# Moving one modulation group of a two-block network from TensorE to VectorE, with earlier loads of the output slabs

## The chip, the cores and the metric

The kernel runs on one core of a Trainium2 chip. The metric is the device time of one execution in microseconds (us); less is better. Engines are named as the profile names them: PE is TensorE, DVE is VectorE, ACT is ScalarE, POOL is GpSimd, SP is SyncE, whose queue issues nearly all loads. In the views, L113 is the line of a helper through which almost every compute operation is recorded, so operations are told apart by the tiles they write and read (out<-in).

## The reference, cut to what matters

512 positions of 1024 channels pass through two blocks, all in fp32. The change lies in the first block, which is conditioned on a vector c:

```python
c_act = jax.nn.silu(c)
cond = c_act @ ada_w[i] + ada_b[i]
shift1, scale1, gate1, shift2, scale2, gate2 = jnp.split(cond, 6, axis=-1)
h = modulate(rmsnorm(x, norm1_g[i]), shift1, scale1)
z = h @ w_in[i] + b_in[i]
...
y = concatenate([rmsnorm(y_a, out_norm_a_g[i]), rmsnorm(y_b, out_norm_b_g[i])])
x = x + gate1 * (y @ w_out[i])
h2 = modulate(rmsnorm(x, norm2_g[i]), shift2, scale2)
g_ff, up_ff = split(h2 @ w_ffn_in[i], 2)
x = x + gate2 * ((silu(g_ff) * up_ff) @ w_ffn_out[i])
shift_f, scale_f = split(c_act @ ada_f_w + ada_f_b, 2)
return modulate(rmsnorm(x, norm_f_g), shift_f, scale_f)
```

The modulation vectors are products of one row (c_act, 1024) with a 1024 x 1024 matrix each. y_a is the spatial gating half of the mixer, y_b the convolution half (width 31, then a norm per channel group and silu). The second block (attention, pooling, two more feed-forward layers) is not touched.

## The kernel before, in words

**Products.** Every fp32 weight slab of 512 KB is loaded into a raw tile, split into a high part (wh, ScalarE) and a low part (wl, VectorE), and each product runs as three matmuls (wh with the high activations, wh with the low ones, wl with the high ones). `Weights` (L284 to L336) holds the plan of slabs: `load` (L296) issues the load on SyncE's queue, `take` gives the next split slab and splits ahead so that four are ready.

**Modulation.** Six groups of 8 slabs (each 128 x 1024 fp32, 512 KB) remain after the first norm: gate1, shift2, scale2, gate2, and the two of the last norm. `ada_fetch(n)` (L631) issues loads until n slabs are waiting. There are two ways to compute a group:

- `ada_group(ahead)` (L649), on TensorE: per slab four fp32 products in the program, which the profile lists as 8 matmul instructions (128x32 weights, 128x256 moving), 64 for a group, into one of the four PSUM banks `mm`; then `ada_columns` turns the row into columns by two transposes; then it fetches up to `ahead` slabs.
- `ada_slab(ahead=4)` (L663), on VectorE: per slab two 128x512 multiply-adds into the accumulator `adac`; after the eighth slab a short product with a matrix of ones (8 matmul instructions) and the same transposes.

**The stage around the change.** After the spatial gating (L1184), gate1 is computed by `ada_group` (L1188). The output projection is then made in two halves. The first-half products (L1193 to L1203) take the four channel blocks of y_a, for each of 8 output blocks m over all 512 positions; `gated` (L1179) scales each with gate1 and adds it to x on VectorE, which frees its `mm` bank. Between them `pump` issues the rest of the convolution: its taps, then centre, norm and silu of y_b, which go back and forth between VectorE, TensorE and ScalarE. At m = 2 shift2 and at m = 5 scale2 are computed by `ada_group`. The second-half products (L1214 to L1238) take y_b, whose operand tiles `HO.put(4 + k, ...)` (L1211) come last out of the convolution; they run over 256 positions at a time and use slabs 4 to 7 of `w_out`. scale2 is needed by `normed` (L534), near the end of this stage.

The feed-forward loop `Ffn.run` (L1091) then makes units m = 3 to 14 over all positions, and after each calls `ada_rest` (L1260), which works off two slabs of the last three groups by `ada_slab`.

**Order.** The program text gives the order of priority. The tile framework's scheduler (`tile.TileContext(nc, auto_bufs=True)`) works out each engine's instruction order from it and from its own estimates, chooses where in on-chip memory each tile lies, and makes a load wait until the last user of that place is done. [...]

Of the kernel before, what the change touches and what calls it, by code (L numbers as in the profile page):

```python
# [42 lines left out]
ADN = 10  # L43
# [77 lines left out]
def body(ctx: ExitStack, tc: tile.TileContext, I: dict, out, dbg=None):  # L121
# [12 lines left out]
    def A(name, dt=F32):  # L134
        tag, bufs = TAGS.get(name, ("m", NB))
        return ar.tile([P, 2, S], dt, tag=tag, name=name, bufs=bufs)
# [13 lines left out]
    def MM():  # L150
        return ps.tile([P, S], F32, tag="mm", name="mm", bufs=4)

    def ST():
        return ps.tile([P, S], F32, tag="st", name="st", bufs=2)
# [15 lines left out]
    def stt(o, a, s, b, op0, op1):  # L170
        return V.scalar_tensor_tensor(o, a, s, b, op0=op0, op1=op1)
# [4 lines left out]
    def ts(o, a, s, op, s2=None, op2=None):  # L176
        if op2 is None:
            return V.tensor_scalar(o, a, s, None, op0=op)
        return V.tensor_scalar(o, a, s, s2, op0=op, op1=op2)

    def dump(name, tiles):
        if dbg is not None and name in dbg:
            for k, t in enumerate(tiles):
                nc.sync.dma_start(dbg[name][:, k, :], t)
# [153 lines left out]
    W = Weights(4)  # L338
# [274 lines left out]
    def pump(n, m=0):  # L613
        owed[0] += n
        owed[1] += m
        n, m = int(owed[0]), int(owed[1])
        owed[0] -= n
        owed[1] -= m
        for j in range(max(n, m)):
            if j < m and bp:  # L620
                bp.popleft()()
            if j < n and bg:
                bg.popleft()()
# [7 lines left out]
    def ada_fetch(n):  # L631

        while adaq and len(adal) < n:
            w, c0, col, bias, k = adaq.popleft()
            a = A("adaw")
            nc.sync.dma_start(a.rearrange("p a c -> p (a c)"), w[k * P:(k + 1) * P, c0:c0 + D])
            adal.append((a, col, bias, k))

    def ada_columns(pq, col, bias):

        sb = T("adasb")
        act(sb[:, :HS], pq[:, :HS], AF.Copy)
        pt = ST()
        for t in range(2):
            TE.transpose(pt[:, t * P:(t + 1) * P], sb[:, t * P:(t + 1) * P], ident)
        v = pt[:, :HS].rearrange("p (t j r) -> p j t r", t=2, j=4)[:, :, :, 0]
        tt(mod[:, col:col + 8].rearrange("p (j t) -> p j t", t=2), v, vecs[bias[0]][:, bias[1]:bias[1] + 8].rearrange("p (j t) -> p j t", t=2), OP.add)

    def ada_group(ahead):  # L649

        pq = MM()
        for k in range(KD):
            ada_fetch(1)
            a, col, bias, _ = adal.popleft()
            for j in range(4):
                TE.matmul(pq[32 * j:32 * j + 32, :HS], lhsT=c32[:, k, :], rhs=a[:, j // 2, (j % 2) * HS:(j % 2 + 1) * HS],
                          start=(k == 0), stop=(k == KD - 1))
        ada_columns(pq, col, bias)
        ada_fetch(ahead)
# [3 lines left out]
    def ada_slab(ahead=4):  # L663

        ada_fetch(1)
        if not adal:
            return
        a, col, bias, k = adal.popleft()
        if k == 0:
            adac[0] = A("adac")  # L670
        acc = adac[0]
        for j in range(2):
            if k == 0:
                ts(acc[:, j], a[:, j], cact[:, k:k + 1], OP.mult)
            else:
                stt(acc[:, j], a[:, j], cact[:, k:k + 1], acc[:, j], OP.mult, OP.add)
        ada_fetch(ahead)
        if k == KD - 1:
            pq = ST()
            for j in range(4):  # L680
                TE.matmul(pq[32 * j:32 * j + 32, :HS], lhsT=ones[:, :32], rhs=acc[:, j // 2, (j % 2) * HS:(j % 2 + 1) * HS], start=True, stop=True)
            ada_columns(pq, col, bias)
# [242 lines left out]
    def factor(acc_, bank=ST):  # L925

        rsb = ACC()
        act(rsb, stats(acc_, 0, S, 512, bank=bank), AF.Copy)
        return rsb
# [243 lines left out]
    def out_mm(o, k0, slab, e, c0, c1):  # L1173
        wh, wl, _ = slab
        cs = slice(e * P, (e + 1) * P)
        for k in range(4):
            HO.mm3(o, k0 + k, wh[:, k, cs], wl[:, k, cs], c0, c1, k == 0, k == 3)

    def gated(m, o, c0, c1, rsb, eng):  # L1179
        t = T()[:, :c1 - c0]  # L1180
        stt(t, o, mod[:, 16 + m:17 + m], rsb[:, c0:c1], OP.mult, OP.mult)
        eng.tensor_tensor(x_(m, c0, c1), x_(m, c0, c1), t, op=OP.add)

    spatial(0, S)  # L1184
    dump("ya", uT)
    for n in (ADN, 0):
        if n:
            ada_group(n)  # L1188
        for _ in range(3):
            pump(PU[4], PP[4])  # L1190
    gets = lazy(1)
    oa = []
    for m in range(KD):  # L1193
        oa.append(MM())
        out_mm(oa[m], 0, gets(m // 2)[0], m % 2, 0, S)
        if m == LA:
            fa = factor(accA)
        if m >= LA:
            for x in range(0 if m == LA else m, m + 1):
                gated(x, oa[x], 0, S, fa, G if GA else V)  # L1200
        pump(PY, PP[5])
        if m in (2, 5):
            ada_group(ADN if m == 2 else 2)  # L1203
    pump(len(bg))
    g2 = C(KD)
    stt(g2, mod[:, 32:40], 1.0, vecs["norm2"], OP.add, OP.mult)
# [51 lines left out]
        yield from normed(HO, sums, c0, c1, ng2[:, 0, 0], None)  # L1258

    def ada_rest(last):  # L1260
        ada_slab()
        ada_slab()
        while last and (adal or adaq):
            ada_slab()

# [44 lines left out]
    def first_kv():  # L1310
        nx["head"] = deque(partial(kv, m, *HALVES[0]) for m in range(4))
    plain_ffn(f1, mod[:, 40:48], to_block2, ada_rest, first_kv)
    dump("xf", [x_(k) for k in range(KD)])
    for m in range(4):
# [466 lines left out]
```

## Time and profile before

| | |
|---|---|
| Median of 3 runs | 1670.14 us (1670.02 to 1671.48) |
| The profiled execution's own time | 1667.07 us |
| its span, first to last instruction | 1665.3 us |
| TensorE matmul busy / weight loads busy | 1627.4 us / 1358.9 us |
| VectorE, ScalarE, GpSimd busy | 881.8, 681.8, 129.5 us |
| Mean granted TensorE clock | 0.993 |

The profiled execution is 3.07 us under the median and has 1.8 us around its span. Busy time of TensorE counts modelled ends of pipelined matmuls, so a busy engine is not one at its peak; a gap, however, is a gap. The views used are the page, busy time by stretch, the chain of waits (what the last instruction waited for, followed back), the timeline of one engine, and the list of who waited for whom.

### The profile page before, as it was taken

Reading aid. Unit: us, or ns where it says so; the run is one execution under the profiler, and the core shown is the slowest. Engines: PE = TensorE matmul, PEld = TensorE weight load, DVE = VectorE, ACT = ScalarE, POOL = GpSimd, SP = SyncE. Lnnn points to the kernel's source line nnn. Section 1 sums busy time; section 2 is a strip of 40 time slices with the busy share of each in tenths; the row PEclk is TensorE's granted clock in tenths of the full one; section 3 lists DMA queues with packets and bytes.
Section 4 is the critical chain, followed back from the end, with each engine's and each line's share of the span. In section 5 each row is a group of like instructions: output and inputs, shape, how many; then the busy total and the mean of one; then the engine's idle time right before and its main releaser. Section 6 shows DMA issues by size and latency. Waiting matters only on the chain.

```text
span 1665.3 us, 22096 instructions
## 1 busy us (share of the span) xinstructions
PE 1627.4 (98%) x8797; PEld 1358.9 (82%) x8797; DVE 881.8 (53%) x1645; ACT 681.8 (41%) x1232; POOL 129.5 (8%) x144
## 2 busy tenths in 40 slices
PE   7999899999999999999999999999999999999998
PEld 5776698887888998777778988888888998888886
DVE  5799585444333584678857344423257734432144
ACT  4585352222222364455658233213237823232232
POOL 0452000000000001100001000000013100000002
PEclk9999999999999999999999999999999999999999
DMA  9635435544531423311144232234134232232411
GB/s 306 179 111 193 152 112 175 154 149 133 153 101 54 120 57 90 90 26 52 39 107 124 61 111 61 95 114 144 59 102 114 77 89 77 83 121 93 121 64 51
DMA packets 245168, 179.55 MB, mean 108 GB/s; under 512 B 20688, under 2 KB 220224, under 8 KB 245064
## 3 DMA queue, kind: packets, MB, share of 16 engines
q1 hardware_dynamic: 240520, 176.99, 36.3%
q10 hardware_dynamic: 4544, 1.14, 0.4%
q8 instruction: 69, 1.13, 0.3%
q14 instruction: 35, 0.29, 0.1%
HBM read 175.99 MB, written 2.11 MB: 107 GB/s over the span
## 4 chain that ended last, share of the span: by engine, by line
PE 86%; DVE 3%; ACT 2%; issue 0%; DMA 0%; SPq 0%; DVEq 0%; ACTq 0%
PE mm L113 79%; PE ax L113 4%; PE st L113 3%; DVE pw L113 1%; ACT sq L113 0%; DMA raw<-in_w_out_dram 0%; ACT pw L113 0%; DVE XT L113 0%; DVE wl L113 0%; DVE sq L113 0%; ACT wh L113 0%; ACT H L113 0%; DVE pt L113 0%; DVE fk L113 0%; DVE mg L113 0%
## 5 line engine op out<-in xcount | busy, mean ns | idle before, releaser
L113 PE MATMUL mm<-H,wh 128*128 128x512 f32 (+1 forms) x3168 | 869.8, 361 | 9.2 <-ACT wh L113 3.4
L113 PEld LDWEIGHTS mm<-H,wh 128*128 128x128 f32 x3168 | 564.1, 189 | 104.5 <-issue 4.4
L113 PE MATMUL mm<-H,wl 128*128 128x512 f32 (+1 forms) x1584 | 567.7, 359 | 2.9 <-DVE wl L113 2.9
L113 DVE TENSOR_TENSOR wl<-raw,wh 128x1024 fp32r<-128x1024 f32 (+1 forms) x257 | 310.4, 1223 | 217.0 <-ACT wh L113 203.2
L113 PEld LDWEIGHTS mm<-H,wl 128*128 128x128 f32 x1584 | 299.3, 189 | 47.7 <-DVE wl L113 3.5
L113 ACT ACTIVATE wh<-raw 128x1024 fp32r<-128x1024 f32 (+1 forms) x257 | 262.5, 1041 | 127.3 <-PE mm L113 52.8
L113 PE MATMUL mm<-wh,hid 128*128 128x512 f32 x704 | 217.3, 389 | 0.0
L113 DVE TENSOR_TENSOR silu<-silu,mm 128x512 f32<-128x512 f32 (+1 forms) x77 | 47.0, 611 | 250.0 <-PE mm L113 243.5
L113 PEld LDWEIGHTS mm<-wh,hid 128*128 128x128 f32 x704 | 132.1, 188 | 27.1
L113 ACT ACTIVATE hid<-silu 128x512 fp32r<-128x512 f32 (+1 forms) x77 | 43.8, 569 | 242.5 <-DVE silu L113 234.9
L113 PE MATMUL mm<-wl,hid 128*128 128x512 f32 x352 | 137.3, 390 | 0.0
L113 PE MATMUL mm<-hid,wh 128*128 128x512 f32 (+1 forms) x464 | 116.4, 340 | 0.0
L113 PEld LDWEIGHTS mm<-hid,wh 128*128 128x128 f32 x464 | 80.3, 190 | 9.9 <-issue 0.4
L113 POOL TENSOR_TENSOR mg<-mg,gb 128x512 f32<-128x512 f32 x32 | 44.3, 1389 | 464.6 <-ACT sq L113 456.0
L113 ACT ACTIVATE silu<-silu 128x512 f32<-128x512 f32 (+1 forms) x52 | 29.3, 565 | 123.1 <-DVE silu L113 123.0
L113 PE MATMUL mm<-hid,wl 128*128 128x512 f32 (+1 forms) x232 | 79.1, 341 | 0.0
L113 PEld LDWEIGHTS mm<-wl,hid 128*128 128x128 f32 x352 | 66.1, 188 | 14.0 <-DVE wl L113 0.3
L113 DVE TENSOR_TENSOR silu<-mm,rsb 128x512 f32<-128x512 f32 (+1 forms) x52 | 31.6, 608 | 73.0 <-PE mm L113 72.5
L113 PE MATMUL mm<-wh,H 128*128 128x512 f32 (+2 forms) x256 | 67.0, 350 | 1.6 <-ACT wh L113 1.6
L113 DVE TENSOR_TENSOR hid<-silu,hid 128x512 fp32r<-128x512 f32 (+1 forms) x77 | 47.3, 614 | 37.4 <-ACT hid L113 37.3
L113 POOL TENSOR_TENSOR cv<-cv,tap 128x488 f32<-128x488 f32 (+12 forms) x40 | 52.5, 1348 | 88.2 <-ACT cv L113 71.2
L113 ACT ACTIVATE silu<-mm 128x512 f32<-128x512 f32 (+1 forms) x25 | 13.7, 546 | 108.7 <-PE mm L113 108.7
(271 smaller groups left out, 1624.7 us busy)
## 6 DMA issues: line engine op xcount, KB each, us to landing
adaw<-in_ada_w_dram SPq DMA_DIRECT2D x48, 512.0 KB
raw<-in_w_ffn_in_dram SPq DMA_DIRECT2D x44, 512.0 KB
raw<-in_ffn_w_gate_dram SPq DMA_DIRECT2D x44, 512.0 KB
raw<-in_ffn_w_up_dram SPq DMA_DIRECT2D x44, 512.0 KB
raw<-in_ffn_w_down_dram SPq DMA_DIRECT2D x44, 512.0 KB
raw<-in_w_in_dram SPq DMA_DIRECT2D x16, 512.0 KB
adaw<-in_ada_f_w_dram SPq DMA_DIRECT2D x16, 512.0 KB
raw<-in_attn_w_in_dram SPq DMA_DIRECT2D x16, 512.0 KB
```

The lines of the kernel that those rows point to most:

```text
L113: ins = f(*a, **k)
```

## The change

gate1's group leaves 8 slabs waiting instead of 10, and four `W.load()` stand before it, so that slabs 4 to 7 of `w_out` are loaded ahead of shift2's slabs. shift2 stays on TensorE at m = 2 and fetches four slabs after it. scale2 is computed by eight `ada_slab` calls, two after each of m = 3 to 6, with 4, 4, 4, 4, 3, 2, 2, 2 slabs kept waiting. `ada_rest` works off three slabs for each feed-forward unit instead of two, so the 24 slabs end with the eighth unit instead of the twelfth.

```diff
     spatial(0, S)
     dump("ya", uT)
-    for n in (ADN, 0):
+    for n in (1, 0):
         if n:
-            ada_group(n)
+            for _ in range(4):
+                W.load()
+            ada_group(8)
         for _ in range(3):
             pump(PU[4], PP[4])
...
         pump(PY, PP[5])
-        if m in (2, 5):
-            ada_group(ADN if m == 2 else 2)
+        if m == 2:
+            ada_group(4)
+        if 3 <= m < 7:
+            for x in range(2):
+                ada_slab(min(4, max(2, 13 - 2 * m - x)))
     pump(len(bg))
...
     def ada_rest(last):
-        ada_slab()
-        ada_slab()
+        for _ in range(3):
+            ada_slab()
         while last and (adal or adaq):
             ada_slab()
```

## Rows read from the trace of the kernel before

**Rows 1.** The page: the span and the engines' busy time.

```profile
span 1665.3 us, 22096 instructions
PE 1627.4 (98%) x8797; PEld 1358.9 (82%) x8797; DVE 881.8 (53%) x1645; ACT 681.8 (41%) x1232; POOL 129.5 (8%) x144
```

**Rows 2.** TensorE's timeline: start, duration, what, xcount, idle before and its releaser.

```profile
172.62 1.05 PE L113 MATMUL mm<-adaw,fixed 128*32 128x256 f32 x10
...
189.42 1.07 PE L113 MATMUL mm<-adaw,fixed 128*32 128x256 f32 x16
...
198.91 0.93 PE L113 MATMUL mm<-H,wh 128*128 128x256 f32 x3 [3.41 <-ACT wh L113]
...
395.51 0.64 PE L113 MATMUL st<-adac,fixed 128*32 128x256 f32 x8
```

**Rows 3.** Chain of waits, 180 to 200 us: start, length, what.

```profile
190.83 6.95 DMA raw<-in_w_out_dram
...
197.80 1.06 ACT wh L113
```

**Rows 4.** SyncE's queue, 120 to 200 us: start, duration, loads issued.

```profile
130.90 7.69 SPq L636 DMA_DIRECT2D adaw<-in_ada_w_dram  x8
138.68 1.71 SPq L309 DMA_DIRECT2D raw<-in_w_out_dram  x2
...
178.36 12.42 SPq L636 DMA_DIRECT2D adaw<-in_ada_w_dram  x8
190.83 0.97 SPq L309 DMA_DIRECT2D raw<-in_w_out_dram  x2
```

**Rows 5.** SyncE's waits, 140 to 180 us: total, times, longest (us).

```profile
SPq L636 <- DVE X L113: 37.9, 1, 37.9
```

**Rows 6.** Stretch: length, busy PE, PEld, DVE, ACT, POOL; clock, DMA share, GB/s.

```profile
155.00:165.00 10.00, 9.53 (x75) 5.81 (x74) 8.28 (x15) 0.86 (x2) 0.00 (x0) 1.00 0.00 0
165.00:175.00 10.00, 10.00 (x77) 6.31 (x77) 5.87 (x11) 2.75 (x5) 0.00 (x0) 1.00 0.01 2
175.00:182.00 7.00, 7.00 (x45) 5.41 (x40) 6.46 (x10) 6.46 (x9) 0.00 (x0) 1.00 0.38 117
182.00:191.00 9.00, 8.49 (x88) 5.61 (x86) 1.28 (x3) 2.10 (x4) 0.00 (x0) 1.00 0.79 298
...
182.00:186.00 4.00, 4.00 (x39) 2.91 (x38) 0.46 (x1) 0.85 (x1) 0.00 (x0) 1.00 1.01 401
...
199.00:202.00 3.00, 3.00 (x11) 2.64 (x12) 1.45 (x2) 1.83 (x4) 0.00 (x0) 0.50 0.63 159
...
230.00:577.00 347.00, 344.14 (x1742) 291.72 (x1740) 156.48 (x210) 100.36 (x137) 0.00 (x0) 1.00 0.45 129
```

**Rows 7.** VectorE's timeline, columns as in Rows 2.

```profile
167.02 0.69 DVE L113 TENSOR_TENSOR z<-cv,st 128x512 f32<-128x512 f32 x1 [1.35 <-PE st L113]
...
181.72 0.75 DVE L113 SCALAR_TENSOR_TENSOR H<-cv,fixed,H 128x512 fp32r<-128x512 f32 x1
...
191.47 0.17 DVE L113 TENSOR_TENSOR fixed<-st,fixed 128x8 f32<-128x8 f32 x1 [3.32 <-PE st L113]
...
270.79 0.69 DVE L113 TENSOR_TENSOR silu<-silu,mm 128x512 f32<-128x512 f32 x1 [7.89 <-PE mm L113]
271.39 0.88 DVE L113 TENSOR_SCALAR adac<-adaw,fixed 128x512 f32<-128x512 f32 x2
...
272.79 6.71 DVE L113 SCALAR_TENSOR_TENSOR adac<-adaw,fixed,adac 128x512 f32<-128x512 f32 x10
281.67 0.69 DVE L113 TENSOR_TENSOR silu<-silu,mm 128x512 f32<-128x512 f32 x1 [2.17 <-PE mm L113]
```

**Rows 8.** The feed-forward loop's late units: timelines of SyncE, VectorE, TensorE.

```profile
360.21 10.79 SPq L636 DMA_DIRECT2D adaw<-in_ada_f_w_dram  x2
...
383.54 2.35 DVE L113 TENSOR_TENSOR wl<-raw,wh 128x1024 fp32r<-128x1024 f32 x2
...
384.81 0.50 PE L113 MATMUL mm<-H,wl 128*128 128x512 f32 x1 [2.86 <-DVE wl L113]
```

## The prediction

> **What bounds the kernel now.** I read the page first, then the stretches around the changed lines, then the timelines there. The page shows TensorE busy for 1627.4 of 1665.3 us [rows 1]: time can be won only by taking work off TensorE or by closing one of its gaps, and a slower VectorE costs something only where TensorE ends up waiting for it. In TensorE's timeline between 145 us and 577 us (the output products and the first feed-forward layer) two gaps are over one microsecond. The first is 3.41 us before 198.91 [rows 2]. The chain of waits gives its cause: a load of `w_out` took 6.95 us, then ScalarE split it in 1.06 us, then the product ran [rows 3]. SyncE's queue says why the load was late: eight modulation slabs stood in front of it from 178.36 on, and the two last `w_out` slabs went out at 190.83 [rows 4]. The first of those eight had itself blocked the queue for 37.9 us, waiting for its place in memory [rows 5]. [...] The second gap is 2.86 us before 384.81, behind two low-part splits on VectorE that began only at 383.54 [rows 8]; I come back to it.
>
> **Removed: scale2 on TensorE.** Its 64 matmuls run in seven pieces, the first of 10 at 172.62, the last of 16 at 189.42 [rows 2]. From the start of each piece to the start of the next other work (the last one to its end) I count 0.98, 0.56, 0.57, 0.57, 0.64, 0.57 and 1.07 us: **5.0 us**. Instead, TensorE gets one product with ones, 8 instructions, 0.64 us at 395.51 [rows 2]: **+0.6**. The two transposes and the evacuation stay, wherever they fall.
>
> **Moved: `w_out` slabs 4 to 7 ahead of shift2's slabs.** Four loads stand before six slab fetches, where eight fetches and then two loads stood [rows 4]. The transfers are ten in both cases. At 401 GB/s [rows 6] one takes 1.3 us, so shift2's last slab lands about four transfers, 5 us, later. TensorE works shift2 off as filler until shortly before scale2's first piece at 172.62 [rows 2], over 30 us after the last of these loads went out [rows 4], so this costs nothing; without that cover it would be up to 1.3 us a slab. The last `w_out` slabs then go out some 60 us before the 198.91 at which they were missing. The 3.41 us gap goes: **3.4**. With it goes the low clock: 3 us at 0.50 is **1.5** us of lost work. Next late at that point are VectorE's `gated` steps; VectorE is busy 1.45 of the 3 us after the gap [rows 6], so I put nothing there.
>
> **Added: sixteen products on VectorE.** Ten in a row take 6.71 us, so a multiply-add costs 0.66 us in a row, and the two opening multiplications cost 0.88 together [rows 7]: 14 x 0.66 + 0.88 is 10.1 us. From 155 to 182 us VectorE is busy 8.28 + 5.87 + 6.46 = 20.6 of 27 us, idle 6.4; from 182 to 191 it is idle 7.7 of 9 [rows 6]. scale2 is not needed before some 216 us. What matters is the convolution's chain, which ends with the operand write at 181.72 [rows 7], just when TensorE begins the second half. The chain has five VectorE steps after its centre, such as the subtraction that begins when TensorE releases it at 167.02 [rows 7]. The lower bound of the cost is zero: the products fill waits of that kind. The upper bound is all sixteen ahead of the last write, 10.1 less 6.4 idle = 3.7. Five steps that each find a product half done give 5 x 0.33 = 1.7. The products stand ahead of the later blocks in the program, so I go above that: **+2.5**.
>
> [...]
>
> scale2's last three pieces also filled TensorE's wait for the norm factor of y_b: 0.64 + 0.57 + 1.07 = 2.3 us. One more output block, 12 matmuls, can be pulled forward into the wait, and scale2's `mm` bank is free for it; 39 matmuls go in 4.0 us there [rows 6], so it fills 1.2 us. The rest stays open: **+1.1**, with bounds of 0 and 2.3.
>
> **Three slabs for each unit.** The last slab is used at unit 10 instead of 14. The gap at 384.81 sits in unit 14: SyncE spent 10.79 us from 360.21 on two fetches, with weight loads behind them, and VectorE then had products before the late splits [rows 8]. With no slabs left there I take the gap as gone: **2.9** (bounds 0 and 2.9). In units 3 to 10 VectorE does six products (4.0 us) beside two splits of 1.2 us [rows 8] and two steps of 0.7, 7.8 us of a unit, which lasts 10.9 from one silu step to the next (270.79 to 281.67) [rows 7]. The DMA engines are at 0.45 [rows 6] and get half as many slabs again there. Cost of the denser fetching: from nothing to a gap like that one in some unit; I take half a gap, **+1.5**. GpSimd's queue has nothing in this stage [rows 6] and is not passed.
>
> **Sum**, against the profiled execution's 1667.07 us: -5.0 - 3.4 - 1.5 - 2.9 + 0.6 + 2.5 + 1.1 + 1.5 = -7.1, so 1660.0. The median of the runs is 1670.14; the same difference there gives **1663.0**.
>
> **Rivals.**
> *All of it hidden* (chance 0.14): the three last costs are zero, -12.8 + 0.6 = -12.2, 1657.9. For it: VectorE's idle time; against: the chain ends without slack.
> *A slab is late and VectorE stands behind it* (0.14). The first fetch for scale2 issued at 178.36 before, after the 37.9 us wait [rows 5]. If the new fetches get such a place, eight transfers of 1.3 us from 178.4 end near 189, the last products near 190.5, and if the operand write of 181.72 is ordered behind them it comes some 9 us later. Then 9.0 replaces the 2.5, TensorE loses the 1.5 of clock again, and the net is +0.9: 1671.0, no change. The trace has the pattern: VectorE stood idle 3.32 us before 191.47, waiting for TensorE's transposes of scale2 [rows 7], with ready work behind. Against: the loads behind which memory was short are now issued earlier, and the wait ended with a VectorE step that may come earlier too.
> [...]
> *The loads don't get ahead* (0.10): the scheduler puts the four loads behind fetches anyway. The 3.4 and 1.5 stay: -2.2, 1667.9, no change.
> *Weight loads fall behind the fetches in the feed-forward loop, and it is slower* (0.12). Place: SyncE's queue in units 3 to 10, three fetches each waiting for VectorE to free a slab. Price: 2.9 us per unit that stalls. Without the 1.5 above the net is -8.6, so three stalls are even, four cost 2.9 us more than before, and with five it is clearly slower: +5.9, 1676.0. For it: the 10.79 us for two fetches [rows 8]. Against: 344.14 of 347 us busy in that loop [rows 6], a single gap in twelve units.
>
> **How the numbers follow.** The forecast has 0.50; with its terms at their bounds it reaches from 1657.9 to 1666.9 (-12.8 + 0.6 + 3.7 + 2.3 + 2.9). About 0.2%, 3.3 us, is what a measurement can tell here. Faster: forecast and full hiding, 0.64. Same: late slab and loads not ahead, 0.24. Slower: 0.12. The range runs from the best case to the late slab, 1657.5 to 1672, and leaves out the stalled loop.
>
> **What would show it.** Right: no gap before the second half's third slab and a clock of 1.00 there; all four late `w_out` loads issued before 145 us; 16 more products on VectorE before 200 us; TensorE starting 256-wide products at most 3 us later than 181.7; no gap in unit 14. Wrong: VectorE idle ahead of a product waiting for a slab, or gaps of 2 to 3 us behind wl in several of units 3 to 10.

## The result: slower by 0.5%

The changed kernel's median is 1678.29 us (five executions, 1676.30 to 1681.19), against 1670.00 us for the kernel before in the same comparison: 1.0051 times as long, 95% interval 1.0039 to 1.0062. A sixth execution took 3366.94 us and is left out of these numbers. Measured again later beside the experiments it gave 1677.18 us, 1.0049 (1.0037 to 1.0062). The forecast was 1663.0 us, with a range up to 1672.0: wrong in sign, and outside the range. The profiled execution took 1679.27 us.

One execution stands behind each profile, and executions of one kernel spread by some microseconds: the profiled one of before (1667.07 us) lies 3.8 us under that kernel's median of 1670.91 us over 35 executions in the first set of experiments. So the table below has a ratio over all executions of a kernel beside two landmarks of its one trace, which tell where a difference arises. Both are on VectorE: the silu step of the first full feed-forward unit, at 270.79 us before [rows 7], which closes the stage around the change, and the first reciprocal after the feed-forward layer (rs<-sd, 128x2), at 578.35 us before and 587.18 us after.

The page after, span and engines, answers to [rows 1]:

```profile
span 1677.5 us, 22012 instructions
PE 1633.5 (97%) x8741; PEld 1364.1 (81%) x8741; DVE 890.7 (53%) x1661; ACT 681.0 (41%) x1232; POOL 130.0 (8%) x144
```

TensorE has 56 instructions fewer (64 less 8) and VectorE 16 more, as the change says; yet TensorE's busy time is 6.1 us longer. The stretches show why (length, busy PE, PEld, DVE, ACT, POOL; clock, DMA share, GB/s; [rows 6] answers to them). First the one stretch of before that [rows 6] leaves out, then after:

```profile
191.00:199.00 8.00, 4.10 (x29) 3.49 (x29) 4.79 (x13) 1.62 (x3) 0.00 (x0) 1.00 0.97 291
```

```profile
165.00:175.00 10.00, 10.00 (x75) 5.66 (x74) 4.65 (x6) 3.54 (x5) 0.00 (x0) 1.00 1.03 412
175.00:182.00 7.00, 7.00 (x60) 5.86 (x60) 6.12 (x11) 3.88 (x5) 0.00 (x0) 1.00 0.21 81
182.00:191.00 9.00, 4.26 (x20) 3.47 (x19) 8.82 (x14) 4.91 (x8) 0.00 (x0) 0.70 0.32 89
191.00:199.00 8.00, 4.42 (x18) 2.49 (x19) 6.80 (x12) 2.39 (x3) 0.00 (x0) 0.50 1.16 295
199.00:202.00 3.00, 3.00 (x15) 3.00 (x16) 2.91 (x5) 0.00 (x0) 0.00 (x0) 0.50 0.69 172
```

From 182 to 191 us VectorE went from 1.28 to 8.82 us busy and TensorE from 8.49 to 4.26. The granted clock is 0.50 through the next two stretches, where before it was 1.00 in the first and 0.50 only in the last 3 us. SyncE's queue after (start, duration, loads issued) answers to [rows 4], and its longest wait between 120 and 160 us to [rows 5]:

```profile
122.08 30.72 SPq L309 DMA_DIRECT2D raw<-in_w_out_dram  x8
155.03 32.39 SPq L636 DMA_DIRECT2D adaw<-in_ada_w_dram  x16
```

```profile
SPq L309 <- DVE uT L113: 18.8, 1, 18.8
```

All eight `w_out` loads now stand in one row, but they need 30.7 us: one of them waits 18.8 us until VectorE has done with the tile uT, whose place in memory it takes. shift2's six remaining slabs, which went out from 130.90 us on before, and scale2's eight go out from 155.03 us. VectorE's timeline after shows what that and the order of the program make of it ([rows 7]):

```profile
176.07 0.74 DVE L113 SCALAR_TENSOR_TENSOR t<-mm,fixed,acc 128x512 f32<-128x512 f32 x1
...
177.94 0.48 DVE L113 TENSOR_SCALAR adac<-adaw,fixed 128x512 f32<-128x512 f32 x1
...
187.65 0.74 DVE L113 SCALAR_TENSOR_TENSOR t<-mm,fixed,acc 128x512 f32<-128x512 f32 x1
188.31 0.74 DVE L113 SCALAR_TENSOR_TENSOR adac<-adaw,fixed,adac 128x512 f32<-128x512 f32 x1
...
191.56 0.74 DVE L113 SCALAR_TENSOR_TENSOR t<-mm,fixed,acc 128x512 f32<-128x512 f32 x1
...
193.49 2.07 DVE L113 SCALAR_TENSOR_TENSOR adac<-adaw,fixed,adac 128x512 f32<-128x512 f32 x3
...
197.97 0.74 DVE L113 SCALAR_TENSOR_TENSOR t<-mm,fixed,acc 128x512 f32<-128x512 f32 x1
...
198.70 0.74 DVE L113 SCALAR_TENSOR_TENSOR H<-cv,fixed,H 128x512 fp32r<-128x512 f32 x1
...
199.97 0.74 DVE L113 SCALAR_TENSOR_TENSOR H<-cv,fixed,H 128x512 fp32r<-128x512 f32 x1
```

The sixteen products (adac) lie between 177.94 and 195.6 us, in among the gated steps (t<-mm) of blocks 5 to 7 and ahead of the last operand writes (H<-cv), which come at 198.70 and 199.97 instead of 180.44 and 181.72. TensorE waits mostly for these gated steps (its timeline after; the wait and its releaser in brackets; [rows 2]):

```profile
183.85 0.50 PE L113 MATMUL mm<-H,wh 128*128 128x256 f32 x2 [1.53 <-ACT H L113]
...
185.33 1.56 PE L113 MATMUL ax<-fixed,acc 128*128 128x1 f32 x8 [0.97 <-DVE acc L113]
188.45 0.80 PE L113 MATMUL mm<-H,wh 128*128 128x256 f32 x2 [1.56 <-DVE t L113]
...
192.36 0.79 PE L113 MATMUL mm<-H,wh 128*128 128x256 f32 x2 [2.05 <-DVE t L113]
...
195.04 1.64 PE L113 MATMUL st<-adac,fixed 128*32 128x256 f32 x8 [0.82 <-DVE adac L113]
...
198.77 0.80 PE L113 MATMUL mm<-H,wh 128*128 128x256 f32 x2 [0.92 <-DVE t L113]
...
358.74 0.50 PE L113 MATMUL mm<-H,wl 128*128 128x512 f32 x1 [2.86 <-DVE wl L113]
```

"DVE t" is a gated step: it frees an `mm` bank. Of the 8.3 us that TensorE idles between 182 and 199 us, 4.53 are put down to the three gated steps and none to the two late operand writes on VectorE ("ACT H" is an operand write on ScalarE). The 3.41 us gap before the third slab is gone, as forecast. The 2.86 us gap of the feed-forward loop [rows 8] is not: it has moved from 384.81 to 358.74. By the landmarks the changed kernel is 274.70 - 270.79 = 3.9 us behind at the first unit and 587.18 - 578.35 = 8.8 us behind after the layer. The profiled execution loses 3.4 us more by its end (spans: 12.2); the later profile, span 1675.1, lost 9.8 in all and 7.9 by the second landmark.

### The profile page after: what moved, and what is told of

It is laid out like the page before. It is cut to its first block, busy times and chain, and to the rows that moved or that the text cites. A ratio compares the mean times of both kernels' runs of the same rounds, so it can differ in the third digit from the quotient of the medians.

```text
span 1677.5 us, 22012 instructions
## 1 busy us (share of the span) xinstructions
PE 1633.5 (97%) x8741; PEld 1364.1 (81%) x8741; DVE 890.7 (53%) x1661; ACT 681.0 (41%) x1232; POOL 130.0 (8%) x144
## 2 busy tenths in 40 slices
DMA packets 245167, 179.53 MB, mean 107 GB/s; under 512 B 20688, under 2 KB 220224, under 8 KB 245064
## 4 chain that ended last, share of the span: by engine, by line
PE 84%; DVE 4%; ACT 2%; issue 1%; DMA 0%; ACTq 0%; POOL 0%; DVEq 0%; POOLq 0%
PE mm L113 78%; PE ax L113 3%; PE st L113 3%; DVE pw L113 1%; DVE wl L113 1%; DMA misc<-in_fox_b_f_dram 0%; ACT sq L113 0%; ACT pw L113 0%; DVE adac L113 0%; DVE XT L113 0%; DVE t L113 0%; ACT L113 0%; ACT XT L113 0%; DVE sq L113 0%; DVE pt L113 0%
```

## The experiments

Two slabs a unit unless three are named; the ratio is an estimate from all executions of a kernel and of the kernel before that ran beside it, with its 95% interval, and need not be the quotient of two medians; the landmarks are in us against the one trace of before. They carry the spread of single executions: e3 and e14 change nothing in the program ahead of the first landmark and stand at +0.9 and +1.4 there, and e15 stands 2.5 us under e1 there, though the two programs differ only behind it.

| run | what is in it | median us | ratio | at 270.79 | at 578.35 |
|---|---|---|---|---|---|
| e1 | early loads alone | 1665.05 | 0.9970 (0.9959 to 0.9982) | -2.1 | -0.7 |
| e2 | group move alone | 1667.49 | 0.9981 (0.9970 to 0.9993) | -2.1 | -0.6 |
| e3 | three a unit alone | 1672.92 | 1.0009 (0.9996 to 1.0022) | +0.9 | +4.2 |
| e4 | loads and group | 1672.59 | 1.0012 (1.0001 to 1.0023) | +3.5 | +5.1 |
| e5 | group and three | 1670.58 | 1.0003 (0.9993 to 1.0013) | -2.5 | +3.6 |
| all three | the changed kernel again | 1677.18 | 1.0049 (1.0037 to 1.0062) | +3.0 | +7.9 |
| e6 | e4, products behind the operand writes | 1681.40 | 1.0073 (1.0060 to 1.0086) | +12.5 | +15.3 |
| e7 | e4, products spread over the second half | 1673.49 | 1.0023 (1.0014 to 1.0033) | +3.4 | +5.0 |
| e16 | e4, products cut to 64 columns | 1665.51 | 0.9967 (0.9954 to 0.9980) | -2.9 | -1.2 |
| e17 | e4, operand writes first | 1671.39 | 1.0008 (0.9997 to 1.0018) | +1.9 | +3.4 |
| e18 | e2, operand writes first | 1665.61 | 0.9975 (0.9962 to 0.9987) | -1.7 | +1.1 |
| e20 | e2, whole chain first | 1665.82 | 0.9977 (0.9966 to 0.9988) | -2.6 | -1.0 |
| e21 | e4, whole chain first | 1668.34 | 0.9992 (0.9981 to 1.0003) | +1.4 | +1.4 |
| e22 | changed kernel, whole chain first | 1672.39 | 1.0021 (1.0009 to 1.0032) | +2.2 | +7.1 |
| e14 | e3, three slabs kept waiting | 1670.84 | 1.0002 (0.9994 to 1.0010) | +1.4 | +3.6 |
| e15 | e1, three slabs kept waiting | 1662.96 | 0.9959 (0.9943 to 0.9975) | -4.6 | -5.2 |

### Each part alone, and two together

```diff
 e1 (on before)
         if n:
+            for _ in range(4):
+                W.load()
             ada_group(n)
...
 e3 (on before)
-        ada_slab()
-        ada_slab()
+        for _ in range(3):
+            ada_slab()
 e2 (on the changed kernel; e4 is the second hunk alone)
-            for _ in range(4):
-                W.load()
...
-        for _ in range(3):
-            ada_slab()
+        ada_slab()
+        ada_slab()
```

> Only the four earlier loads of w_out; scale2 stays on TensorE and two slabs a unit stay. Theory O (the order on VectorE: sixteen products ahead of gated steps and operand writes made the output stage late): without the products the early loads do what they were meant to, the 3.4 us gap and the 1.5 us of low clock after it go, 1664 to 1667 us. Theory L (the early loads themselves: the fifth waits for its place in memory and holds the modulation slabs behind it in SyncE's queue to 155 us): the output stage is late here as well, 1673 to 1676 us, with shift2's and scale2's slabs issued from 155 us on and gaps of TensorE between 158 and 200 us.

> Only scale2's move to VectorE, without the earlier loads and with two slabs a unit. Theory O: the sixteen products stand ahead of the second pair of operand writes here too, those come 10 us or more later than 180.4 and 181.7, and the output stage costs some 5 us as in the changed kernel: 1673 to 1676 us. Theory L: shift2's slabs come as early as before, the products find VectorE's idle time, TensorE is rid of 5.0 us of scale2: 1664 to 1668 us.

> Only three slabs for each feed-forward unit instead of two. Theory T (three a unit stall units by themselves): some 5 us more between 230 and 400 us, with gaps behind a silu step or a late split in units 9 and 10, 1673 to 1677 us. Rival (the loop only inherits the lateness of the output stage): the unit-14 gap of 2.9 us goes and nothing comes in its place, 1666 to 1669 us.

> The changed kernel with two slabs a unit as before. Theory T: the 5 us that the changed kernel loses between 232 and 406 us come back, 1673 to 1675 us. Rival (the loop inherits the lateness): no gain, 1678 to 1682 us, with the late-unit gap back at unit 14.

Theories O and L each said that one of the two edits in the output stage is bad by itself. Neither is: the loads alone win 0.30%, the group's move alone 0.19%. Together they lose 0.12% where the product of the two would be 0.9951. By the first landmark it is 3.5 us instead of -4.2. Part of that distance is no interaction: e2 keeps `ada_group(8)`, which leaves 8 slabs waiting instead of 10, and its last `w_out` loads went out from 181.05 us instead of 190.83, so both edits close the same 3.41 us gap and it can be won only once. Counting those 3.4 us once (-0.8 instead of -4.2), the pair still ends 4.3 us behind. In e1 the queue is as in the changed kernel, with the modulation slabs from 156 us on, and between 182 and 202 us TensorE has one gap over 0.3 us left, 0.69 us. In e2 (TensorE's timeline) there is one gap, for an operand write:

```profile
191.46 0.58 PE L113 MATMUL mm<-H,wh 128*128 128x256 f32 x1 [6.28 <-DVE H L113]
```

and that costs less than the 5.0 us of scale2 and the `w_out` gap that go. What differs between e2 and e4 is how many gated steps stand behind products. In e2 those of blocks 5 and 6 ran at 178.15 and 179.53 us, before the first product at 180.20; in e4 they ran at 187.66 and 191.57, among the products. VectorE's timelines, e2 and then e4:

```profile
179.53 0.74 DVE L113 SCALAR_TENSOR_TENSOR t<-mm,fixed,acc 128x512 f32<-128x512 f32 x1
180.20 0.87 DVE L113 TENSOR_SCALAR adac<-adaw,fixed 128x512 f32<-128x512 f32 x2
```

```profile
187.66 0.74 DVE L113 SCALAR_TENSOR_TENSOR t<-mm,fixed,acc 128x512 f32<-128x512 f32 x1
```

Theory T fell between the two ends given: three a unit alone is 1.0009 times as long, not told from no change, but its trace is 4.2 us behind at the second landmark where the forecast had a gain.

### Do they add up?

> The changed kernel without the four earlier loads (group move and three slabs a unit). The single edits gave 0.9970 (loads), 0.9981 (group) and 1.0009 (three a unit) of the time before, loads and group together 1.0012. Theory I (what is bad is the loads and the group together: late slabs, products in one row ahead of gated steps and operand writes): without the loads the two remaining edits add up, 0.9981 and 0.0009 to 0.0030 for three a unit, so 1667 to 1673 us. Rival (the group's move and three a unit also hurt each other): 1675 us or more.

> The changed kernel once more, beside the others on one chip. If the single edits and this run are measured alike, 1.0051 of the time before comes out again, 1678 to 1680 us; if part of it was the chip or the low-clock stretch near 1266 to 1285 us in its profile, 1673 to 1677 us.

e5 is the changed kernel without the four loads, `after_again` the changed kernel unaltered. Without the loads the other two add up: three a unit adds 0.0022 to e2's 0.9981, and 0.0009 (-0.0004 to 0.0022) when alone. So it is loads and group together that are bad, and three a unit costs on top; to e4 it adds 0.0037. The repetition gave 1.0049, so the first 1.0051 stands.

### Is it the products' time on VectorE, or the late slabs?

```diff
 e16 (on e4)
-                stt(acc[:, j], a[:, j], cact[:, k:k + 1], acc[:, j], OP.mult, OP.add)
+                w = 64 if col == 32 else S
+                stt(acc[:, j, :w], a[:, j, :w], cact[:, k:k + 1], acc[:, j, :w], OP.mult, OP.add)
```

> Early loads, scale2 on VectorE, two slabs a unit, but the fourteen multiply-adds of scale2 take 64 of 512 columns (scale2 is wrong by that in most columns); every slab is still fetched, in the same order of SyncE's queue. Theory O (it is the time and the place of the products on VectorE): some 8 us of VectorE go from in front of the gated steps and the operand writes, TensorE no longer waits there, 1660 to 1664 us. Rival L (the late slabs cost it, whatever is done with them): 1670 to 1674 us, as with full products.

0.9967, against 1.0012 with whole products, with the slabs as late (the transfers from 155 to 165 us ran at 318 GB/s; in the changed kernel, whose 16 fetches begin at 155.03 us, at 359; in e2, without the early loads, there were none) and the queue in the same order: the products' time is what counts, and rival L falls as the direct cause. VectorE's order moved a little too: block 5's gated step ran after six products, at 182.39 us, in e4 after eight. The time misses theory O's figures, and it is no better than that of the early loads alone (0.9970), though scale2 has left TensorE: three waits of over 0.5 us remain (e16, TensorE's timeline).

```profile
185.53 0.63 PE L113 MATMUL mm<-H,wh 128*128 128x256 f32 x3 [0.81 <-ACT H L113]
...
186.71 1.05 PE L113 MATMUL ax<-fixed,acc 128*128 128x1 f32 x8 [0.56 <-DVE acc L113]
...
189.40 0.80 PE L113 MATMUL mm<-H,wh 128*128 128x256 f32 x2 [1.64 <-DVE t L113]
```

### Does it help to move the products, or what they delay?

```diff
 e6 (on e4): the products leave the first half's loop; g2, which needs scale2,
 moves behind them
         HO.put(4 + k, yb[k], 0, S, scale=vecs["onb"][:, k:k + 1])
+    for k in range(KD):
+        ada_slab(min(4, max(2, 7 - k)))
 e7 (on e4): instead of that, in the second half's loop
             out_mm(ob[m][:, :HS], 4, slabs[m // 2], m % 2, c0, c1)
+            if c0 == 0:
+                ada_slab(min(4, max(2, 7 - m)))
```

> Early loads and scale2 on VectorE, two slabs a unit, but the sixteen products stand behind the four y_b operand writes in the program, so VectorE does the gated steps of blocks 5 to 7 and the operand writes first. Theory O (the order on VectorE is what cost the output stage): the writes come near 184 us again, TensorE does not wait for them, scale2's 5.0 us are won, and the gap before the third slab is closed: 1660 to 1664 us. Rival L (the slabs that the early loads delay cost it anyway): 1669 to 1674 us as with the two edits together. New risk: sixteen products in a row, 10 us, now stand ahead of the second half's gated steps, which hold mm banks; that would be some 4 us of TensorE waiting between 188 and 202 us, 1665 to 1668 us.

> As the run with the products behind the operand writes, but one slab's two products after each of the eight output blocks of the second half's first pass. Theory O: 1659 to 1663 us, the best of the set, since neither operand writes nor gated steps wait for a long row of products. Rival L: 1669 to 1674 us. If the row of products still forms in VectorE's order behind the first gated steps, it lies between the two, 1663 to 1667 us.

The operand writes came early (187.78 and 189.04 us in e6), but theory O's figures fell with a new wait. In both, VectorE did all sixteen products in one row. e6, VectorE's timeline:

```profile
200.26 0.88 DVE L113 TENSOR_SCALAR adac<-adaw,fixed 128x512 f32<-128x512 f32 x2
201.05 9.36 DVE L113 SCALAR_TENSOR_TENSOR adac<-adaw,fixed,adac 128x512 f32<-128x512 f32 x14
```

and TensorE, whose own order has the short product with ones next, waited for its end (e6, TensorE's timeline):

```profile
209.89 1.64 PE L113 MATMUL st<-adac,fixed 128*32 128x256 f32 x8 [15.28 <-DVE adac L113]
```

In e7 the same wait was 7.68 us, at 214.18. The "new risk" that e6's text priced at 4 us was the outcome, and larger. The row is not the whole of it in e6: it began 5.7 us after TensorE had stopped, and before it VectorE stood idle for 4.65 and 1.12 us in front of weight splits that waited for ScalarE. Nor is SyncE's queue that of e4 here: the last six of the sixteen fetches went out behind four loads of `w_ffn_in`, from 189.04 us in e6 and 198.72 in e7, so these two runs move slabs as well as products.

```diff
 e17 (on e4) and e18 (on e2)
-        HO.put(4 + k, yb[k], 0, S, scale=vecs["onb"][:, k:k + 1])
+        with tc.high_priority(offset=1000) if k > 1 else nullcontext():
+            HO.put(4 + k, yb[k], 0, S, scale=vecs["onb"][:, k:k + 1])
 e20 (on e18), e21 (on e17), e22 (e21 with three a unit): the same priority also for
     the first half's gated(x, oa[x], ...), fb = factor(accB, AXP),
     and gated(x, ob[x][:, :HS], ...) while c0 == 0
```

> The same with full products, and the last two operand writes alone put ahead of twelve of the products in VectorE's order (a higher priority for them); SyncE's queue is the same. Theory O in the form 'the operand writes are late': they come near 185 instead of 199 us and the time falls to 1662 to 1665 us. Theory O in the form 'the gated steps that free the mm banks are late': the banks of blocks 5 to 7 still come free at 188, 192 and 198 us, TensorE has only some 24 more matmuls to do between these, 3 us, 1668 to 1671 us. Rival L: no gain, 1671 to 1674 us.

> Scale2 on VectorE without the early loads, and the same priority for the last two operand writes. Without it this kernel took 0.9981 of the time before and TensorE stood 6.28 us before 191.5 us for such a write. If that gap is worth its length, 1660 to 1662 us; if the gated steps behind the row of products hold the banks next, the gap only shrinks or moves, 1664 to 1667 us.

In e17 the two writes run from 183.55 us, 15 us earlier than in e4, and it gains 0.04%, inside the intervals. So the late operand writes by themselves were not what cost e4 its time. The median, 1671.39 us, lies in rival L's figures; the trace speaks for the second form of theory O: TensorE still waits 3.43 us in sum for the gated steps at 190.50, 194.41 and 200.25, which hold the banks, and 2.37 us for a sum of squares (acc). e17, VectorE's timeline and then TensorE's:

```profile
183.55 1.41 DVE L113 SCALAR_TENSOR_TENSOR H<-cv,fixed,H 128x512 fp32r<-128x512 f32 x2
```

```profile
188.18 1.59 PE L113 MATMUL ax<-fixed,acc 128*128 128x1 f32 x8 [2.37 <-DVE acc L113]
191.30 0.79 PE L113 MATMUL mm<-H,wh 128*128 128x256 f32 x2 [1.53 <-DVE t L113]
```

In e18 the 6.28 us gap went and the next wait came, for the norm factor's reciprocal, which stood behind nine products; 0.9975 is no different from 0.9981. e18, VectorE's timeline and then TensorE's:

```profile
183.93 5.38 DVE L113 SCALAR_TENSOR_TENSOR adac<-adaw,fixed,adac 128x512 f32<-128x512 f32 x8
...
190.37 0.74 DVE L113 SCALAR_TENSOR_TENSOR adac<-adaw,fixed,adac 128x512 f32<-128x512 f32 x1
...
191.63 0.17 DVE L113 RECIPROCAL rs<-sd 128x4 f32<-128x4 f32 x1
```

```profile
191.94 2.04 PE L113 MATMUL ax<-fixed,rs 128*128 128x128 f32 x8 [4.80 <-DVE rs L113]
```

> Scale2 on VectorE without the early loads, with a higher priority for all that TensorE waits for in this stage: the first half's gated steps, the last two operand writes, the norm factor of y_b and the first-pass gated steps of the second half. In the run with the writes alone put first (0.9975) TensorE then stood 4.80 us before 191.9 us for a reciprocal of that factor, which lay behind nine products, and the clock was low for 10 us after. Theory O: that wait shrinks to 1 to 2 us and the low clock to some 3 us, 1659 to 1663 us. Rival (the row of eleven products only holds the next step, the gated step of block 7): 1664 to 1668 us.

> Early loads and scale2 on VectorE, two slabs a unit, with the same priorities; SyncE's queue is that of the two edits without them (1.0012), only VectorE's order differs. Theory O: 1660 to 1665 us, at or under the early loads alone (0.9970). Rival L (the late slabs): 1670 to 1673 us.

> The changed kernel itself with the same priorities, three slabs a unit. Theory O: the output stage gives back 6 to 10 us of the changed kernel's 1.0049; the feed-forward loop still loses its 3 to 6 us: 1666 to 1671 us. Rival L: 1675 to 1679 us.

e21 does better than e4 (0.9992 against 1.0012, intervals that just touch) and e22 better than the changed kernel (1.0021 against 1.0049, intervals apart) with SyncE's queue in the same order as theirs; so part of the loss is VectorE's order. All three miss theory O's figures, e22 only just. e20, without the loads, is not told from e2 or e18 (0.9977 against 0.9981 and 0.9975), and its time lies in its rival's figures: the reciprocal ran early, at 186.52 us, and TensorE waits 6.30 us for the products instead (e20, TensorE's timeline):

```profile
194.91 1.64 PE L113 MATMUL st<-adac,fixed 128*32 128x256 f32 x8 [6.30 <-DVE adac L113]
```

The wait moved in e21 as well: block 7's gated step ran at 199.58, behind eleven products, and TensorE waited for these (e21, TensorE's timeline):

```profile
191.32 2.08 PE L113 MATMUL ax<-fixed,rs 128*128 128x128 f32 x8 [1.43 <-DVE rs L113]
198.01 1.64 PE L113 MATMUL st<-adac,fixed 128*32 128x256 f32 x8 [4.62 <-DVE adac L113]
```

Five orders (e4, e6, e7, e17, e21) of the same sixteen products between 177 and 215 us left TensorE waiting 6 us or more in sum between 182 and 217 us, in e4 and e17 mostly for gated steps, in e6, e7 and e21 mostly for the end of the row; only making them short (e16, 3.2 us of waiting) brought the time down to that of the early loads alone.

### The feed-forward loop

```diff
 e14 (on e3) and e15 (on e1)
-    def ada_slab(ahead=4):
+    def ada_slab(ahead=3):
```

> Three slabs a unit as in the run of that edit alone (1.0009), with three slabs kept waiting instead of four; VectorE's order then has no products between a unit's silu step and the late splits behind it. If those products are what makes the 2.86 us gap before 355.7 us there, the gap goes and 3 to 4 us with it: 1667 to 1669 us. If the gap comes from late weight loads, it stays: 1671 to 1674 us.

> The early loads alone, with three slabs kept waiting instead of four in the feed-forward loop; VectorE's order then has no two products between the silu step and the late splits of unit 14. If those products make the 2.86 us gap of that unit, 1661 to 1663 us; if another wait takes its place, 1664 to 1666 us as with the loads alone (0.9970).

The loop between the silu steps of its first and last full unit, as one stretch: before, then e3 (columns as above).

```profile
270.79:395.62 124.83, 121.97 (x552) 99.25 (x554) 66.31 (x91) 31.12 (x42) 0.00 (x0) 1.00 0.53 159
```

```profile
271.64:400.89 129.25, 125.11 (x559) 99.78 (x558) 68.14 (x94) 34.20 (x47) 0.00 (x0) 1.00 0.53 158
```

TensorE's idle time rises from 124.83 - 121.97 = 2.86 us, the one gap, to 4.14; the other 3.14 us by which the stretch is longer are busy time. e3's timeline of TensorE has the three pieces:

```profile
340.58 0.70 PE L113 MATMUL mm<-H,wh 128*128 128x512 f32 x2 [0.94 <-DVE silu L113]
341.62 0.50 PE L113 MATMUL mm<-H,wl 128*128 128x512 f32 x1 [0.34 <-DVE wl L113]
...
355.66 0.50 PE L113 MATMUL mm<-H,wl 128*128 128x512 f32 x1 [2.86 <-DVE wl L113]
```

In the changed kernel the gap has this make-up: ten products in a row (the first two, at 346.28, are not shown), VectorE idle until the unit's silu step, two products, and only then the splits (VectorE's timeline):

```profile
347.08 5.38 DVE L113 SCALAR_TENSOR_TENSOR adac<-adaw,fixed,adac 128x512 f32<-128x512 f32 x8
355.53 0.69 DVE L113 TENSOR_TENSOR silu<-silu,mm 128x512 f32<-128x512 f32 x1 [3.07 <-PE mm L113]
356.14 1.41 DVE L113 SCALAR_TENSOR_TENSOR adac<-adaw,fixed,adac 128x512 f32<-128x512 f32 x2
357.46 2.35 DVE L113 TENSOR_TENSOR wl<-raw,wh 128x1024 fp32r<-128x1024 f32 x2
```

In e14 and e15 the two products no longer stand there. e15's gap shrank from 2.86 us (e1) to 1.53, about the 1.41 us that two products last; e14 lost the 2.86 us gap but got three of 0.5 us in the following unit, and its ratio of 1.0002 is not told from e3's 1.0009: missed. The rest of the 3 us of three a unit is only partly accounted for. The ones products are one candidate: e3 makes two of its three in two pieces of four, 0.6 us each, where eight in one piece take 0.64 us [rows 2]. That was not isolated.

e15 is the best kernel of the study: 1662.96 us, 0.9959 (0.9943 to 0.9975), faster than both kernels, with scale2 left on TensorE. Its interval overlaps e1's, and 2.5 us of its lead in the traces lie before the loop, where its edit changes nothing; so it is not shown that three kept waiting adds to the early loads.

## Why the prediction was wrong

**What bounds the kernel** held in the output stage: time was lost where TensorE waited, and a share of 53% on VectorE said nothing of it. In the feed-forward loop waits explain only a part of the loss, as told below.

**Removed, scale2 on TensorE, -5.0**: the matmuls are gone (64 less 8), but no run measures the 5.0 by itself. e2 and e16 are faster than before, but in both the gap before the third slab went as well, and e16 is no faster than e1, which keeps scale2 on TensorE.

**`w_out` first, -3.4 and -1.5**: the gap went in every run with the loads. That part was right. But the step said that shift2's slabs would land four transfers, 5 us, later and that "this costs nothing". They went out 24 us later, since one load had to wait 18.8 us for its place, and the queue held all behind it; the eight loads were out at 152.8 us and not before 145. I had that kind of wait in front of me, 37.9 us in [rows 5], and counted transfers. The price was not quite nothing: without shift2's matmuls as filler a wait for a gated step grew from 0.47 to 1.53 us, in the changed kernel and in e1 alike (TensorE's timeline, before and then after). Alone the loads still won 0.30% (e1).

```profile
160.08 0.73 PE L113 MATMUL mm<-H,wh 128*128 128x512 f32 x2 [0.47 <-DVE t L113]
```

```profile
158.70 0.73 PE L113 MATMUL mm<-H,wh 128*128 128x512 f32 x2 [1.53 <-DVE t L113]
```

**Added, sixteen products, +2.5 with an upper bound of 3.7**: this is the step that failed. It set the products against VectorE's idle time from 155 to 182 us and took the last operand write as the only thing that could be late. Three things were wrong in it. The products were not there to fill that idle time: the first ran at 177.94. The chain was not the only customer: gated steps free banks, the norm factor's reciprocal and the ones product stood behind products too, and in the changed kernel it was the gated steps that TensorE waited for. And the write was not late by 3.7 us at most, but by 199.97 - 181.72 = 18.3; yet that lateness was not the cost in e4, as e17 shows, which won 15 us of it back and 0.04% of the time. The sum up to the first unit was -5.0 - 3.4 - 1.5 + 0.6 + 2.5 + 1.1 = -5.7; the trace shows +3.9, the later one +3.0. Cutting the fourteen multiply-adds to an eighth of their columns gives back 6.4 us by the first landmark (e4's +3.5 against e16's -2.9), and 1672.59 - 1665.51 = 7.1 us of median. That is about all the time taken from them: a multiply-add takes 0.20 us in a row in e16, and 14 x (0.67 - 0.20) is 6.6 us. The duration itself was right: 9.36 us for fourteen is 0.67 us each, and 0.66 was taken.

**The clock** went the other way: the 3 us at 0.50 before, from 199 to 202 us [rows 6], became 16 (the five from 186 to 191, then 8 and 3). I had counted on 1.5 us coming back. No run shows that 1.5 by itself, and what the lower clock cost beside the waits no run separates; where the gap went without the products, in e1, the clock from 199 to 202 us was 1.00, but 0.81 from 175 to 182.

**Norm factor, +1.1**: the changed kernel shows no wait for it (the `ax` product ran at 203.84 us without idle time), nor does e20. It was there where products stood in front of the reciprocal, 4.80 us in e18 and 1.43 in e21.

**Three a unit, -2.9 and +1.5**: wrong in sign. "With no slabs left there I take the gap as gone" failed: the 2.86 us gap stands behind a row of products and two more of them, and that row moved to an earlier unit. From the first to the second landmark e3 loses 4.2 - 0.9 = 3.3 us, the changed kernel 4.9 (with a stretch of low clock in it), where -1.4 was forecast. Kernels with two slabs a unit and four kept waiting lose between 0.0 (e21) and 2.8 us (e6, e18) there, so a part of these is spread; but each kernel with three loses more than its partner with two, from 3.3 us (e3 against before, the changed kernel against e4) to 4.9 (e22 against e21). The gaps explain only 1.3 us of e3's.

**The range** had a slip that made no difference: with the late gap at its own bound of 0 the sum reaches 1669.7 us, not 1666.9.

**The rivals.** "A slab is late and VectorE stands behind it" had the right place and a late operand write, by 9 us; but VectorE did not stand idle for a slab, it was busy for 8.82 of 9 us, and the write was not what TensorE waited for. In the changed kernel the first half's products on TensorE end at 180.9 us, and block 5's gated step, ready by then, ran at 187.65, 6.75 us later, behind eight of the modulation products. The slower rival, weight loads behind fetches, had the sign, but not the price or the cause: one gap and two short ones, each put down to VectorE, not five stalled units.

What stays open: what makes up the rest of the 3 us of three a unit, most of which is busy time of TensorE; and why loads and group together leave the gated steps of blocks 5 and 6 behind the products, where the group alone did not. The later slabs moved shift2's matmuls and VectorE's idle time (4.65 of 10 us busy from 165 to 175 us), which fits, but no run changed that alone.

## What to carry to other kernels

Before work is moved to an engine that is half idle, list every step on that engine that another one waits for in the stretch where the work will stand, and treat its whole length as a delay of the first of these that is ordered behind it (here 6.6 us taken from the products gave back 6.4 by the first landmark); the average idle time was no cover here (VectorE was busy for 53% of the span, but for 8.82 of the 9 us from 182 to 191). Edits that each win can lose together when they meet on one engine's order (here 0.9970 and 0.9981 alone, 1.0012 as a pair), so measure them alone and in pairs. Before a load is placed earlier in the queue, ask when its place in memory comes free: here the fifth `w_out` load waited 18.8 us for that, and from 129.61 to 148.43 us the queue issued nothing.

## What the runs showed that was not expected

In the changed kernel many short gaps went with a lower clock for longer than one long gap did in e2. There no gap of TensorE between 185 and 202 us is over 2.05 us, and the granted clock was 0.50 through the 11 us from 191 to 202; TensorE was busy for 4.42 of the first 8 us, in pieces. In e2, with one gap of 6.28 us, it was 0.84 from 182 to 191 us, 0.75 from 191 to 199, and 1.00 after. And SyncE's queue stood for 18.8 us behind one load while the transfer paths were mostly free: from 130 to 148 us after, the DMA share was 0.24.
